# The general path of the experts moved two experts forward and shortened, x added in the last expert's turn, and the second block's tiles 32 bytes lower

## The chip, the cores and the metric

The kernel runs on one core of a Trainium2 chip. The metric is the time of one execution on the device in microseconds (us). It was measured three times before the change: 1717.10, 1709.79 and 1703.56 us, the median being 1709.79 us. One further execution was recorded by the hardware profiler; all rows below come from it.

## The reference: what is computed

The input is a sequence of 256 tokens with 1024 features in 32-bit floats. A first block applies a mixer, attention to a memory and a layer of 32 experts; a second block follows, of four SwiGLU layers ("ffn"), a recurrent layer and an attention layer. What matters here:

```python
for l in range(DEPTH):
    h = rmsnorm(x, norm_mix_g[l])
    x = x + parallel_mixer(h, ...)
    h = rmsnorm(x, norm_mem_g[l])
    x = x + memory_cross_attention(h, ...)
    h = rmsnorm(x, norm_ffn_g[l])
    x = x + hierarchical_moe(h, ...)      # each token: 2 of 32 experts
return rmsnorm(x, final_g)
# second block, D_FF = 2816, four times:
def swiglu(h, w13, w2):
    gate, up = jnp.split(h @ w13, 2, axis=-1)
    return (jax.nn.silu(gate) * up) @ w2
```

## The kernel before, in words

Features lie on partitions, tokens along the free dimension; x is kept as the tile `xT` of 8 chunks of 128 features by 256 tokens. The kernel writes the order of each engine's work out by hand, by the order of the Python statements; a tile framework adds the waits. SyncE's queue (SP) starts all the loads of weights, in program order.

**Products.** Most products are made of three matmuls in a reduced 32-bit format (`mm3`, L179 to L184): each factor is split into a high and a low part, and high by high (L182), high by low (L183) and low by high (L184) are added up. A weight tile of 1 MB (`raw`) is loaded, ScalarE (ACT) rounds it into `wh` (L159), and VectorE (DVE) subtracts that into `wl` (L160). The weights are the stationary operand of these matmuls, and 256 tokens of the activations the moving one: `xgh`/`xgl` are the normalised x, `hh`/`hl` the hidden features of an ffn (two buffers of each, in turn), `xkvh`/`xkvl` and `yh`/`yl` inputs of later layers.

**An ffn** (`ffn`, L1077) runs over 11 pieces of 256 hidden features (F = 2816): 48 matmuls into PSUM `A` from `xgh`/`xgl` (gate), 48 into `B` (up), and 48 from `hh`/`hl` into the sums `acc` (`rowproj`, L338). Four ffn make 4 x 11 x 48 = 2112 matmuls that read `hh` or `hl`.

**The experts** (`experts`, L812) run one after the other. Each has 32 slots for tokens out of each of two halves; its 6 MB of weights come in 6 tiles of 1 MB, 4 of `w_gu` and 2 of `w_down`, through a ring of 16 slots, the last eight loads through the 8 slots `raw` alone. In the turn of expert e TensorE (PE) makes gate and up of e (L938), adds the result of e-2 to the sums (`combine`, L979), transposes (L948) and makes the down product of e-1 (L964). In the turn of expert 24 (`e == NE - 8`), 16 full 32-bit matmuls by the identity (L887) add `xT` to `acc`.

**The general path.** A token can have more slots wanted than there are; then a flag `fi` is set, and a loop over all experts (`moe_over`, L982) computes what is missing. `rest` (L792 to L795) loads the flag on all engines and branches on it; with the inputs used here the path isn't taken. It stands behind the last `combine`. Ahead of it four loads of the second block's first weights are issued (`s.early`), which `wload` later picks up instead of loading.

**After the experts**, `after_moe` (L1025) makes two products of gains (`gg` L1030, `g2` L1032), then `xgh` on ACT (L226) and `xgl` on DVE (L227) out of the sums, with `gg`; then the first ffn starts.

Of the kernel before, what the change touches and what calls it, by code (L numbers as in the profile page):

```python
# [8 lines left out]
F32 = mybir.dt.float32  # L9
F32R = mybir.dt.float32r  # L10
I32 = mybir.dt.int32
AF = mybir.ActivationFunctionType
# [4 lines left out]
P = 128  # L17
T = 256
D = 1024
KC = D // P  # L20
EPS = 1e-6
F = 2816
NE = 32
# [24 lines left out]
class Block:  # L48
    def __init__(s, ctx, tc, io):
        s.tc, s.nc, s.ctx, s.io = tc, tc.nc, ctx, io  # L50
        s.n = s.turn = 0
        s.queue = s.behind = None
        s.early = []
        pool = lambda name, bufs, **k: ctx.enter_context(tc.tile_pool(name=name, bufs=bufs, **k))
        s.cp = pool("const", 1)
        s.wp = pool("weights", 3)
        s.tp = pool("temps", 2)
        s.xp = pool("x", 1)
        s.pa = pool("acc", 1, space=PSUM)
        s.pp = pool("ps", 2, space=PSUM)  # L60
# [76 lines left out]
    def wload(s, views, C, N, parts=1, between=None):  # L137

        nc = s.nc
        full = C * N == 2048  # L140
        early = s.early.pop(0) if s.early else None
        raw = s.new(s.wp, [P, 2048], "raw", F32, RAW) if early is None else early.rearrange("p c n -> p (c n)")
        wh = s.new(s.wp, [P, 2048], "wh", F32R, WHL)
        wl = s.new(s.wp, [P, 2048], "wl", F32R, WHL)
        v = lambda t: t[:, :C * N].rearrange("p (c n) -> p c n", n=N)
        if not isinstance(views, list):
            n = C // parts
            views = [views[:, i * n:(i + 1) * n] for i in range(parts)]
        c = 0
        for i, view in enumerate(views if early is None else []):  # L150
            nc.sync.dma_start(v(raw)[:, c:c + view.shape[1]], view)
            c += view.shape[1]
            if between is not None:
                between(i)
        cuts = max(parts, 2) if full else parts
        n = C * N // cuts
        for i in range(cuts):
            lo, hi = i * n, (i + 1) * n
            act = nc.scalar.copy(wh[:, lo:hi], raw[:, lo:hi])  # L159
            dve = nc.vector.tensor_sub(wl[:, lo:hi], raw[:, lo:hi], wh[:, lo:hi].bitcast(F32))  # L160
            if s.behind is not None:
                s.after(s.behind[0], act)
                s.after(s.behind[1], dve)
        return v(wh), v(wl)
# [611 lines left out]
        w4 = lambda a: a.unsqueeze(2).unsqueeze(3).to_broadcast(sh4)  # L776
        return pos, gs, gates, over, fi

    def moe(s, mt, xg, st, first):

        nc = s.nc
        s.mt = mt
        y = []

        def rows():
            y.append(s.rstd(s.colsum(st, s.bank()[1][:, 0:2]), D)[1])
            y.append(s.new(mt, [P, 2], "my"))
            nc.vector.tensor_copy(y[1], y[0])
            return y[0]
        pos, gs, gates, over, fi = s.route(xg, rows)  # L790
        with s.tc.tile_pool(name="experts", bufs=1) as me:
            def rest(acc):  # L792

                flag = nc.values_load(fi[0:1, 0:1], min_val=0, max_val=1)
                with s.tc.If(flag > 0):  # L795
                    s.moe_over(over, y[1], acc)
            acc = s.experts(me, pos, gs, gates, rest, first)
        return acc

    def tokens(s, xg, ks):  # L800
# [8 lines left out]
                        s.pe(s.nc.tensor.matmul(pt[:, h, j], src[:, k + j, h * P:(h + 1) * P], s.idr, start=True, stop=True))  # L809
                s.nc.scalar.copy(dst[:, :, k * P:(k + 2) * P], pt.rearrange("p h j b -> p h (j b)"))  # L810

    def experts(s, mt, pos, gs, gates, rest, first):  # L812
        nc = s.nc
        mm = nc.tensor.matmul

# [57 lines left out]
        acc = s.accs()  # L873
        for e in range(NE):
            i = e % 4
            if i == 0:
                now = nxt
                nxt = group(e + 4) if e + 4 < NE else None
            gx, rs = [x[i] for x in now[2]], slot[1][:, 1:2]
            ps = s.expert_in(e, gx)  # L880
            gu = s.new(mt, [P, 512], "gu", F32, 2)
            nc.scalar.mul(gu, ps, rs)
            if done is not None:
                s.combine(acc, *done)
            if e == NE - 8:
                for k in range(KC):
                    s.pe(mm(acc[k // 2][:, k % 2], s.ident, s.xT[:, k], start=False, stop=False))  # L887
            if nxt:
                gather(nxt, 2 * i)
            own = slot  # L890
            if e + 1 < NE:
                slot = slots(nxt if i == 3 else now, e + 1, (i + 1) % 4)
            hx = s.expert_act(mt, gu)
            if prev is not None:
                done = prev[0], s.expert_down(mt, *prev), prev[2]
            prev = (e, hx, *own)
        last = prev[0], s.expert_down(mt, *prev), prev[2]
        s.combine(acc, *done)
        s.combine(acc, *last)
        s.queue = None  # L900
        s.early = [s.wraw(view, KC, 256) for view in first]
        rest(acc)
        return acc

    def expert_loads(s):
# [76 lines left out]
    def moe_over(s, over, y, acc):  # L982

        nc, io, tc = s.nc, s.io, s.tc
        mm = nc.tensor.matmul
        with tc.tile_pool(name="over", bufs=1) as t:
            hT = s.new(s.mt, [P, KC, T], "tokh")
            r = s.spread(y, s.ps([P, T]))
            for k in range(KC):
                nc.vector.scalar_tensor_tensor(hT[:, k], s.xT[:, k], s.col("norm_ffn_g", k), r, op0=ALU.mult, op1=ALU.mult)  # L990
            for b in range(4):
                nc.scalar.copy(s.xT[:, 2 * b:2 * b + 2], acc[b])
            with tc.For_i(0, NE, 1) as e:
                dg = s.tmp([P, 2, P], "dg", 1)
# [4 lines left out]
                gb = s.new(t, [P, T], "ogb")  # L999
                nc.vector.tensor_copy(gb, pb)  # L1000
                row = lambda name, i: io[name][ds(e, 1), i].rearrange("o p c n -> p (o c) n")
                for c in range(4):
                    ps = s.ps([P, 2, T])
                    for n in range(2):
                        for i in range(4):
                            w = s.new(t, [P, 2, P], "ow", F32, 2)
                            nc.sync.dma_start(w, row("w_gu", i)[:, 2 * n:2 * n + 2, c * P:(c + 1) * P])
                            for j in range(2):
                                mm(ps[:, n], w[:, j], hT[:, 2 * i + j], start=i + j == 0, stop=i + j == 4)
                    hf = s.new(t, [P, T], "ohf")  # L1010
                    nc.scalar.activation(hf, ps[:, 0], AF.Silu)
                    nc.vector.tensor_mul(hf, hf, ps[:, 1])
                    nc.vector.tensor_mul(hf, hf, gb)
                    for i in range(2):
                        w = s.new(t, [P, 512], "owd")
                        nc.sync.dma_start(w, row("w_down", c // 2)[:, c % 2, i * 512:i * 512 + 512])
                        for m in range(4):
                            ps = s.ps([P, T])
                            mm(ps, w[:, m * P:(m + 1) * P], hf, start=True, stop=True)
                            nc.vector.tensor_add(s.xT[:, 4 * i + m], s.xT[:, 4 * i + m], ps)  # L1020
            for k in range(KC):
                mm(acc[k // 2][:, k % 2], s.ident, s.xT[:, k], start=k % 2 == 0, stop=k % 2 == 1)


    def after_moe(s, acc, p2):  # L1025


        nc = s.nc
        gg = s.new(p2, [P, KC], "gg")
        nc.vector.tensor_mul(gg, s.col("final_g", 0, 8), s.col("ffn1_norm_2", 0, 8))  # L1030
        g2 = s.new(p2, [P, KC], "g2")
        nc.vector.tensor_mul(g2, s.col("final_g", 0, 8), s.col("final_g", 0, 8))  # L1032
        xg = s.pair(s.xp, KC, "xg")
        for k in range(KC):
# [289 lines left out]
    def run(s):  # L1324
        tc, io = s.tc, s.io
        s.setup()
        with tc.tile_pool(name="first", bufs=1) as p1:
            s.cur = p1
            xg, rows, km, vm = s.mixer(p1)
            xg, st = s.mem_attention(p1, xg, rows, km, vm)  # L1330
        with tc.tile_pool(name="moe", bufs=1) as mt:
            w13 = io["ffn1_w13_2"][0]
            acc = s.moe(mt, xg, st, [w13[j] for j in (0, F // 256, 1, F // 256 + 1)])
# [19 lines left out]
RAW, WHL = 8, 3  # L1353
# [73 lines left out]
```

## Time and profile before

| | |
|---|---|
| median of 3 runs | 1709.79 us |
| the profiled execution | 1704.26 us |
| its span, first to last instruction | 1702.5 us |
| PE busy | 1655.3 us (97%) |
| DVE busy | 927.7 us (54%) |
| ACT busy | 704.4 us (41%) |
| mean granted clock of PE | 0.993 |

The span is the time from the first to the last instruction, 1.8 us less than that execution's own time. The granted clock is the share of full speed that the chip gave TensorE; it has two levels, 1.0 (2.4 GHz) and 0.5 (1.2 GHz). Experts fill about 246 to 709 us of the span, the second block the rest.

### The profile page before, as it was taken

The page shows a single profiled execution, that of the slowest core. Times are in us where ns is not written, and L with a number is a line of the kernel's source. Part 1 is how long each engine was busy: PE and PEld are TensorE (multiplying, and loading weights), DVE is VectorE, ACT ScalarE, POOL GpSimd, SP SyncE. Part 2 cuts the span into 40 slices and gives each one's busy share as a digit, 9 for nine tenths or more (in the row PEclk, how much of TensorE's full clock was granted, in tenths as well). Part 3 has the DMA queues.
Part 4 walks back from the last instruction along what each step waited for, and adds up shares of the span by engine and source line. Part 5 has one row for each costly group of instructions (what it writes and reads, how often), then busy time and mean ns, then how long its engine had stood idle before and what let it go on. Part 6 is the DMA issues. An engine that isn't in the chain of part 4 may idle for free.

```text
span 1702.5 us, 28058 instructions
## 1 busy us (share of the span) xinstructions
PE 1655.3 (97%) x11847; PEld 1350.5 (79%) x11847; DVE 927.7 (54%) x1636; ACT 704.4 (41%) x1138; POOL 5.0 (0%) x19
## 2 busy tenths in 40 slices
PE   8999999999999998799999999999999998999998
PEld 7878984444444443499999999999899997799998
DVE  7998651111111111385558875557655558875554
ACT  8525542111111111344346753436544346764342
POOL 0000000000000000000000000000000000000000
PEclk9999999999999999999999999999999999999999
DMA  9334369999999999865543555554655554135530
GB/s 363 137 124 177 127 251 387 420 419 419 419 420 419 420 420 419 360 264 198 177 158 138 225 215 179 187 186 144 220 182 192 179 192 155 50 125 192 181 123 26
DMA packets 60229, 408.03 MB, mean 240 GB/s; under 512 B 6595, under 2 KB 9923, under 8 KB 11459
## 3 DMA queue, kind: packets, MB, share of 16 engines
q1 hardware_dynamic: 60096, 406.18, 61.9%
q8 instruction: 95, 1.56, 0.4%
q14 instruction: 38, 0.29, 0.0%
HBM read 405.11 MB, written 1.05 MB: 239 GB/s over the span
## 4 chain that ended last, share of the span: by engine, by line
PE 54%; DVE 2%; ACT 1%; issue 0%; POOL 0%; ACTq 0%
PE acc L183 6%; PE A L183 6%; PE A L182 6%; PE acc L182 6%; PE A L184 6%; PE acc L184 6%; PE B L183 6%; PE B L182 6%; PE B L184 6%; DVE wl L160 1%; PE A L1285 1%; PE B L407 0%; ACT wh L159 0%; PE B L190 0%; PE A L190 0%
## 5 line engine op out<-in xcount | busy, mean ns | idle before, releaser
L159 ACT CAST wh<-raw 128x1024 fp32r<-128x1024 f32 (+2 forms) x378 | 377.9, 1035 | 425.5 <-issue 368.6
L160 DVE TENSOR_TENSOR wl<-raw,wh 128x1024 fp32r<-128x1024 f32 (+2 forms) x378 | 448.9, 1205 | 142.8 <-ACT wh L159 141.9
L182 PE MATMUL A<-xgh,wh 128*128 128x256 f32 (+1 forms) x872 | 246.1, 282 | 7.0 <-ACT xgh L226 7.0
L182 PE MATMUL B<-xgh,wh 128*128 128x256 f32 x872 | 245.4, 281 | 6.6 <-ACT wh L159 6.6
L183 PE MATMUL B<-xgl,wh 128*128 128x256 f32 x872 | 245.5, 282 | 0.0
L184 PE MATMUL B<-xgh,wl 128*128 128x256 f32 x872 | 245.5, 281 | 0.0
L183 PE MATMUL A<-xgl,wh 128*128 128x256 f32 (+1 forms) x872 | 245.4, 282 | 0.0
L184 PE MATMUL A<-xgh,wl 128*128 128x256 f32 (+1 forms) x872 | 244.8, 281 | 0.3 <-DVE wl L160 0.3
L183 PE MATMUL acc<-hl,wh 128*128 128x256 f32 x704 | 197.9, 282 | 0.2
L184 PE MATMUL acc<-hh,wl 128*128 128x256 f32 x704 | 197.9, 282 | 0.0
L182 PE MATMUL acc<-hh,wh 128*128 128x256 f32 x704 | 195.0, 282 | 0.1
L182 PEld LDWEIGHTS A<-xgh,wh 128*128 128x128 f32 (+1 forms) x872 | 164.4, 189 | 7.7 <-ACT xgh L226 7.5
L182 PEld LDWEIGHTS B<-xgh,wh 128*128 128x128 f32 x872 | 164.3, 188 | 7.5 <-ACT wh L159 6.9
L184 PEld LDWEIGHTS B<-xgh,wl 128*128 128x128 f32 x872 | 164.2, 188 | 1.5 <-DVE wl L160 0.9
L184 PEld LDWEIGHTS A<-xgh,wl 128*128 128x128 f32 (+1 forms) x872 | 164.3, 188 | 0.5 <-DVE wl L160 0.5
L183 PEld LDWEIGHTS A<-xgl,wh 128*128 128x128 f32 (+1 forms) x872 | 164.3, 188 | 0.5 <-DVE xgl L227 0.4
L183 PEld LDWEIGHTS B<-xgl,wh 128*128 128x128 f32 x872 | 164.4, 189 | 0.3
L848 DVE COPY gx<-B 128x128 f32<-128x128 f32 x64 | 18.6, 291 | 234.0 <-PE B L842 225.7
L938 PE MATMUL A<-raw,gx 128*64 128x512 f32 x560 | 128.0, 596 | 5.8 <-DMA raw<-in_w_gu_dram 5.8
L183 PEld LDWEIGHTS acc<-hl,wh 128*128 128x128 f32 x704 | 132.3, 188 | 0.6 <-DVE hl L225 0.6
L182 PEld LDWEIGHTS acc<-hh,wh 128*128 128x128 f32 x704 | 131.8, 189 | 1.0 <-ACT hh L225 0.7
L184 PEld LDWEIGHTS acc<-hh,wl 128*128 128x128 f32 x704 | 132.2, 188 | 0.0
(408 smaller groups left out, 2372.3 us busy)
## 6 DMA issues: line engine op xcount, KB each, us to landing
raw<-in_ffn_w_dram SPq DMA_DIRECT2D x132, 1024.0 KB, 4.8
raw<-in_w_gu_dram SPq DMA_DIRECT2D x70, 1024.0 KB, 19.9
raw<-in_w_down_dram SPq DMA_DIRECT2D x34, 1024.0 KB, 19.9
wh<-in_w_gu_dram SPq DMA_DIRECT2D x22, 1024.0 KB, 19.9
wl<-in_w_gu_dram SPq DMA_DIRECT2D x22, 1024.0 KB, 19.9
wh<-in_w_down_dram SPq DMA_DIRECT2D x11, 1024.0 KB, 19.9
wl<-in_w_down_dram SPq DMA_DIRECT2D x11, 1024.0 KB, 19.9
raw<-in_a_w_in_dram SPq DMA_DIRECT2D x8, 1024.0 KB, 5.0
```

The lines of the kernel that those rows point to most:

```text
L159: act = nc.scalar.copy(wh[:, lo:hi], raw[:, lo:hi])
L160: dve = nc.vector.tensor_sub(wl[:, lo:hi], raw[:, lo:hi], wh[:, lo:hi].bitcast(F32))
L182: s.pe(mm(out, w[0], x[0], start=first, stop=False))
L183: s.pe(mm(out, w[0], x[1], start=False, stop=False))
L184: s.pe(mm(out, w[1], x[0], start=False, stop=last))
L848: nc.vector.tensor_copy(dst, pg[:, :, i])
L938: s.pe(s.nc.tensor.matmul(ps[g * CAP:(g + 1) * CAP], gx[t // 2][:, 2 * (t % 2) + c], w[:, g, c * 512:c * 512 + 512], start=t + c == 0, sto ...
L1285: mm(sc[:, lo:lo + ke], qT[b:b + 64, c, qb * P:qb * P + P], kT[b:b + 64, c, 0:ke], start=True, stop=True)
```

## The change

1. `rest` is called at the end of the turn of expert 30 (`e == NE - 2`), behind the down product of expert 29, instead of behind the last `combine`. The four early loads vanish; the first loads of the second block are ordinary ones behind the conditional.
2. The general path is written as nested loops with fewer instructions (on PE 156 instead of some 470, counting each 32-bit matmul's two passes and their weight loads), adds into `xT` alone, and no longer copies the sums into `xT` and back.
3. The 16 matmuls that add `xT` to the sums (L884 in the new numbering) stand in the turn of expert 31 (`e == NE - 1`), between `combine` of expert 29 and the transposes. They come after the conditional, so that they carry what it may have added.
4. `g2`, 32 bytes a partition, is made in the pool of temporary tiles (tag `nr8`) and no longer in the pool `second`. Each later tile of `second`, and of the pools stacked on it, lies 32 bytes lower. Start addresses in bytes within a partition, as the two built programs have them:

| tile | before | mod 128 | after | mod 128 |
|---|---|---|---|---|
| hh (two) | 163712, 165760 | 0 | 163680, 165728 | 96 |
| hl (two) | 167808, 169856 | 0 | 167776, 169824 | 96 |
| xkvh, xkvl | 171904, 180096 | 0 | 171872, 180064 | 96 |
| yh, yl | 212960, 221152 | 96 | 212928, 221120 | 64 |
| xgh, xgl | 138816, 147008 | 64 | the same | 64 |
| wh (three) | 77344, 85536, 93728 | 32 | the same | 32 |
| wl (three) | 101920, 110112, 118304 | 32 | the same | 32 |

```diff
@@ wload
-        early = s.early.pop(0) if s.early else None
-        raw = s.new(s.wp, [P, 2048], "raw", F32, RAW) if early is None else early.rearrange("p c n -> p (c n)")
+        raw = s.new(s.wp, [P, 2048], "raw", F32, RAW)
...
@@ moe
-            def rest(acc):
+            def rest():
 
                 flag = nc.values_load(fi[0:1, 0:1], min_val=0, max_val=1)
                 with s.tc.If(flag > 0):
-                    s.moe_over(over, y[1], acc)
-            acc = s.experts(me, pos, gs, gates, rest, first)
+                    s.moe_over(over, y[1])
+            acc = s.experts(me, pos, gs, gates, rest)
@@ experts
-            if e == NE - 8:
+            if e == NE - 1:
                 for k in range(KC):
                     s.pe(mm(acc[k // 2][:, k % 2], s.ident, s.xT[:, k], start=False, stop=False))
...
             prev = (e, hx, *own)
+            if e == NE - 2:
+
+                rest()
+                s.queue = []
         last = prev[0], s.expert_down(mt, *prev), prev[2]
         s.combine(acc, *done)
         s.combine(acc, *last)
         s.queue = None
-        s.early = [s.wraw(view, KC, 256) for view in first]
-        rest(acc)
         return acc
@@ moe_over
-            for b in range(4):
-                nc.scalar.copy(s.xT[:, 2 * b:2 * b + 2], acc[b])
...
+                with tc.For_i(0, 2, 1) as u:
+                    with tc.For_i(0, 2, 1) as c:
+                        part(e, u, c)
...
-            for k in range(KC):
-                mm(acc[k // 2][:, k % 2], s.ident, s.xT[:, k], start=k % 2 == 0, stop=k % 2 == 1)
@@ after_moe
-        g2 = s.new(p2, [P, KC], "g2")
+        g2 = s.tmp([P, KC], "nr8", 1)
```

PE's order at the conditional, before. L979 is the last `combine`, L794 and L795 the flag and the branch, L182 the second block's first matmul; between lies the general path.

```order
L979 MATMUL acc_2782<-oT_5557,yl_5654 128x256
L979 MATMUL acc_2784<-oT_5557,yl_5654 128x256
L794 TENSOR_LOAD fi_2660
L795 COMPARE_AND_BRANCH
...
L1022 MATMUL acc_2781<-xT,ident 128x256 x2
L1022 MATMUL acc_2782<-xT,ident 128x256 x2
L1022 MATMUL acc_2783<-xT,ident 128x256 x2
L1022 MATMUL acc_2784<-xT,ident 128x256 x2
L795 UNCONDITIONAL_BRANCH x2
L182 MATMUL A_6052<-xgh_6034,wh_6054 128x256
L183 MATMUL A_6052<-xgl_6035,wh_6054 128x256
```

After: the conditional stands between the down product of expert 29 (L963) and gate and up of expert 31 (L937), and the `xT` matmuls (L884) two steps behind it.

```order
L963 MATMUL A_5562<-raw_5366,hx_5482 64x512 x4
L963 MATMUL A_5562<-raw_5372,hx_5482 64x512 x4
L791 TENSOR_LOAD fi_2660
L792 COMPARE_AND_BRANCH
...
L792 UNCONDITIONAL_BRANCH
L937 MATMUL A_5719<-raw_5489,gx_5035 64x512 x4
...
L884 MATMUL acc_2781<-xT,ident 128x256 x2
L884 MATMUL acc_2782<-xT,ident 128x256 x2
L884 MATMUL acc_2783<-xT,ident 128x256 x2
L884 MATMUL acc_2784<-xT,ident 128x256 x2
L947 MATMUL A_5762<-ident,gu_5736 128x128 x4
```

So nothing stands any more between the last `combine` and L182, and what follows the branch on PE is now the 16 matmuls of expert 31.

DVE's order at the same place before: `yl` (L969) of the last expert, the first `wl`, the branch, and only then `gg` and the first `xgl`.

```order
L969 SCALAR_TENSOR_TENSOR yl_5641<-A_5631,gt_5481,yh_5640 128x512
L969 SCALAR_TENSOR_TENSOR yl_5654<-A_5644,gt_5559,yh_5653 128x512
L160 TENSOR_TENSOR wl_6055<-raw_5689,wh_6054 128x1024 x2
L794 TENSOR_LOAD fi_2660
L795 COMPARE_AND_BRANCH
...
L795 UNCONDITIONAL_BRANCH x2
L1030 TENSOR_TENSOR gg_6030<-par 128x8
L1032 TENSOR_TENSOR g_1136_6032<-par 128x8
L227 SCALAR_TENSOR_TENSOR xgl_6035<-acc_2781,gg_6030,xgh_6034 128x256
```

After:

```order
L951 TENSOR_TENSOR hx_5560<-sl_5558,A_5553 128x256
L968 SCALAR_TENSOR_TENSOR yl_5576<-A_5562,gt_5407,yh_5575 128x512
L791 TENSOR_LOAD fi_2660
L792 COMPARE_AND_BRANCH
...
L792 UNCONDITIONAL_BRANCH
L1038 TENSOR_TENSOR gg_5834<-par 128x8
L951 TENSOR_TENSOR hx_5769<-sl_5767,A_5762 128x256
L968 SCALAR_TENSOR_TENSOR yl_5781<-A_5771,gt_5473,yh_5780 128x512
L968 SCALAR_TENSOR_TENSOR yl_5794<-A_5784,gt_5551,yh_5793 128x512
L158 TENSOR_TENSOR wl_5860<-raw_5858,wh_5859 128x1024 x2
L225 SCALAR_TENSOR_TENSOR xgl_5839<-acc_2781,gg_5834,xgh_5838 128x256
```

`gg` now follows the branch directly, ahead of the last `hx` and the last two `yl`, and `wl` is followed by `xgl` without a branch between.

SP's order before: the last two loads of the experts, the four early ones, the branch, and the first ordinary load (L151).

```order
L176 DMA raw_5575<-in_w_down_dram 128x2048
L176 DMA raw_5581<-in_w_down_dram 128x2048
L176 DMA raw_5689<-in_ffn_w_2_dram 128x2048
L176 DMA raw_5691<-in_ffn_w_2_dram 128x2048
L176 DMA raw_5693<-in_ffn_w_2_dram 128x2048
L176 DMA raw_5695<-in_ffn_w_2_dram 128x2048
L794 TENSOR_LOAD fi_2660
L795 COMPARE_AND_BRANCH
...
L795 UNCONDITIONAL_BRANCH x2
L794 ISA x2
L151 DMA raw_6361<-in_ffn_w_2_dram 128x2048
```

After:

```order
L174 DMA raw_5567<-in_w_down_dram 128x2048
L174 DMA raw_5573<-in_w_down_dram 128x2048
L791 TENSOR_LOAD fi_2660
L792 COMPARE_AND_BRANCH
...
L792 UNCONDITIONAL_BRANCH
L791 ISA x2
L149 DMA raw_5858<-in_ffn_w_2_dram 128x2048
L149 DMA raw_5914<-in_ffn_w_2_dram 128x2048
```

The first loads of the second block are now issued behind SP's branch, and the branch stands behind the experts' last load as before.

## Rows read from the trace of the kernel before

**Rows 1.** Windows: start and end us, length, busy by engine, granted PE clock, DMA share, GB/s

```profile
core 0: us, PE busy (x) PEld busy (x) DVE busy (x) ACT busy (x) POOL busy (x), PEclk, DMA share, GB/s
640.00:660.00 20.00, 18.44 (x98) 6.61 (x96) 2.27 (x5) 2.82 (x5) 0.00 (x0) 1.00 1.01 421
714.06:720.88 6.82, 5.04 (x22) 4.81 (x23) 4.96 (x15) 5.57 (x13) 0.12 (x1) 0.50 0.66 210
760.00:800.00 40.00, 40.00 (x341) 40.00 (x341) 23.81 (x25) 16.61 (x19) 0.00 (x0) 1.00 0.50 183
246.40:253.20 6.80, 6.07 (x22) 5.07 (x23) 4.98 (x19) 1.07 (x4) 0.00 (x0) 0.50 1.01 418
```

**Rows 2.** Timeline of PE, expert 31 to the second block: start us, us, what, idle before

```profile
687.43 1.94 PE L938 MATMUL A<-raw,gx 128*64 128x512 f32 x8
...
694.83 1.94 PE L938 MATMUL A<-raw,gx 128*64 128x512 f32 x8 [0.56 <-DMA raw<-in_w_gu_dram]
...
698.42 3.65 PE L964 MATMUL A<-raw,hx 128*64 128x512 f32 x16
702.40 1.94 PE L964 MATMUL A<-raw,hx 128*64 128x512 f32 x8 [0.33 <-SPq L795]
704.80 1.94 PE L964 MATMUL A<-raw,hx 128*64 128x512 f32 x8 [0.46 <-SPq L795]
...
708.31 0.73 PE L979 MATMUL acc<-oT,yl 64*128 64x256 f32 x8
715.84 0.58 PE L182 MATMUL A<-xgh,wh 128*128 128x256 f32 x1 [6.79 <-ACT xgh L226]
```

**Rows 3.** Instructions of line L795, the branch, on the sequencers: duration ns min/median/max, start us

```profile
L795 SPq EVENT_SEMAPHORE  x8: 17/17/17, 700.1 to 714.7; - x8
...
L795 PEldq COMPARE_BRANCH  x1: 5672/5672/5672, 709.2 to 709.2; - x1
```

**Rows 4.** DMA queues from 712 to 714 us: packets, MB, share

```profile
q8 instruction: 1, 0.02, 3.4%
```

**Rows 5.** Timeline of DVE around the same places

```profile
688.34 0.75 DVE L969 SCALAR_TENSOR_TENSOR yl<-A,gt,yh 128x512 fp32r<-128x512 f32 x1 [3.48 <-ACT yh L968]
...
708.44 2.36 DVE L160 TENSOR_TENSOR wl<-raw,wh 128x1024 fp32r<-128x1024 f32 x2 [0.18 <-ACT wh L159]
714.98 0.17 DVE L1030 TENSOR_TENSOR gg<-par 128x8 f32<-128x8 f32 x1 [4.18 <-PEq L795]
715.82 1.66 DVE L227 SCALAR_TENSOR_TENSOR xgl<-acc,gg,xgh 128x256 fp32r<-128x256 f32 x4 [0.59 <-ACT xgh L226]
```

**Rows 6.** Timeline of PE at the matmuls that add x (expert 24's turn)

```profile
591.60 3.72 PE L887 MATMUL acc<-xT,ident 128*128 128x256 f32 x16
594.97 0.59 PE L842 MATMUL B<-oh,tokh 128*128 128x256 f32 x2
```

**Rows 7.** Timeline of PE in the second block: starts 48 matmuls apart

```profile
1663.53 0.28 PE L182 MATMUL B<-xgh,wh 128*128 128x256 f32 x1
...
1669.18 0.28 PE L182 MATMUL acc<-hh,wh 128*128 128x256 f32 x1
...
1674.94 0.28 PE L182 MATMUL A<-xgh,wh 128*128 128x256 f32 x1
...
968.38 0.28 PE L182 MATMUL acc<-yh,wh 128*128 128x256 f32 x1
...
973.82 0.28 PE L182 MATMUL acc<-yh,wh 128*128 128x256 f32 x1
```

**Rows 8.** Groups by line, 710 to 1703 us: count, busy us and mean ns, idle before

```profile
L182 PE MATMUL acc<-hh,wh 128*128 128x256 f32 x704 | 195.0, 282 | 0.1
L182 PE MATMUL acc<-yh,wh 128*128 128x256 f32 x64 | 17.7, 276 | 0.0
L182 PE MATMUL acc<-xkvh,wh 128*128 128x256 f32 x64 | 17.5, 300 | 0.0
```

**Rows 9.** Timeline of PE: two gaps in the experts' stretch

```profile
246.53 0.36 PE L737 MATMUL B<-ow,up 128*128 128x32 f32 x1 [2.17 <-DVE w L756]
...
665.06 1.94 PE L938 MATMUL A<-xgl,gx 128*64 128x512 f32 x8 [1.33 <-DMA xgl<-in_w_gu_dram]
```

More of the change, by code (lines that the diff above doesn't have):

```diff
@@ L52, in __init__ @@
         s.queue = s.behind = None
-        s.early = []
         pool = lambda name, bufs, **k: ctx.enter_context(tc.tile_pool(name=name, bufs=bufs, **k))
@@ L149, in wload @@
         c = 0
-        for i, view in enumerate(views if early is None else []):
+        for i, view in enumerate(views):
             nc.sync.dma_start(v(raw)[:, c:c + view.shape[1]], view)
@@ L777, in route, with moe @@
         return pos, gs, gates, over, fi
-    def moe(s, mt, xg, st, first):
+    def moe(s, mt, xg, st):
         nc = s.nc
@@ L810, in tokens, with experts @@
                 s.nc.scalar.copy(dst[:, :, k * P:(k + 2) * P], pt.rearrange("p h j b -> p h (j b)"))
-    def experts(s, mt, pos, gs, gates, rest, first):
+    def experts(s, mt, pos, gs, gates, rest):
         nc = s.nc
@@ L980, in combine, with moe_over @@
                             start=e == 0 and i == 0 and m % 2 == 0, stop=e == NE - 1 and i == 1 and m % 2 == 1))
-    def moe_over(s, over, y, acc):
+    def moe_over(s, over, y):
         nc, io, tc = s.nc, s.io, s.tc
@@ L990, in moe_over, with part @@
                 nc.vector.scalar_tensor_tensor(hT[:, k], s.xT[:, k], s.col("norm_ffn_g", k), r, op0=ALU.mult, op1=ALU.mult)
-            for b in range(4):
-                nc.scalar.copy(s.xT[:, 2 * b:2 * b + 2], acc[b])
+            wg = io["w_gu"].rearrange("e i p n c -> (e i) p n c")
+            wd = io["w_down"].rearrange("e t p c n -> (e t) p c n")
+            gb = s.new(t, [P, T], "ogb")
+            def part(e, u, c):
+                ga = s.new(t, [P, 2, T], "oga")
+                nc.vector.memset(ga, 0.0)
+                with tc.For_i(0, 4, 1) as i:
+                    hk = s.new(t, [P, 2, T], "ohk")
+                    nc.vector.tensor_copy(hk, hT[:, ds(i * 2, 2)])
+                    for n in range(2):
+                        w = s.new(t, [P, 2, P], "ow", F32, 2)
+                        nc.sync.dma_start(w, wg[ds(e * 4 + i, 1), :, 2 * n:2 * n + 2, ds(u * 2 * P + c * P, P)].rearrange("o p n c -> p (o n) c"))
+                        ps = s.ps([P, T])
+                        for j in range(2):
+                            mm(ps, w[:, j], hk[:, j], start=j == 0, stop=j == 1)
+                        nc.vector.tensor_add(ga[:, n], ga[:, n], ps)
+                hf = s.new(t, [P, T], "ohf")
+                nc.scalar.activation(hf, ga[:, 0], AF.Silu)
+                nc.vector.tensor_mul(hf, hf, ga[:, 1])
+                nc.vector.tensor_mul(hf, hf, gb)
+                for i in range(2):
+                    w = s.new(t, [P, 512], "owd")
+                    nc.sync.dma_start(w, wd[ds(e * 2 + u, 1), :, ds(c, 1), i * 512:i * 512 + 512].rearrange("o p c n -> p (o c n)"))
+                    for m in range(4):
+                        ps = s.ps([P, T])
+                        mm(ps, w[:, m * P:(m + 1) * P], hf, start=True, stop=True)
+                        nc.vector.tensor_add(s.xT[:, 4 * i + m], s.xT[:, 4 * i + m], ps)
             with tc.For_i(0, NE, 1) as e:
@@ L998, in moe_over @@
                     mm(pb[:, h * P:(h + 1) * P], s.ones, dg[:, h], start=True, stop=True)
-                gb = s.new(t, [P, T], "ogb")
                 nc.vector.tensor_copy(gb, pb)
[L1001 to L1020, printed above, removed]
-            for k in range(KC):
-                mm(acc[k // 2][:, k % 2], s.ident, s.xT[:, k], start=k % 2 == 0, stop=k % 2 == 1)
+                with tc.For_i(0, 2, 1) as u:
+                    with tc.For_i(0, 2, 1) as c:
+                        part(e, u, c)
     def after_moe(s, acc, p2):
@@ L1331, in run @@
         with tc.tile_pool(name="moe", bufs=1) as mt:
-            w13 = io["ffn1_w13_2"][0]
-            acc = s.moe(mt, xg, st, [w13[j] for j in (0, F // 256, 1, F // 256 + 1)])
+            acc = s.moe(mt, xg, st)
         with tc.tile_pool(name="second", bufs=1) as p2:
```

## The prediction

> **What bounds the kernel now.** I read the windows first, then PE's timeline, then single lines. In the experts' stretch the DMA engines are full (share 1.01, 421 GB/s) and PE waits a little for each weight tile; in the second block PE is busy for 40.00 of 40.00 us at full clock while DMA stands at half [rows 1]. So a microsecond of PE saved among the experts is lost to the next landing, and one saved in the second block comes off the end. Between the two lies the conditional. PE's timeline shows its last combine at 708.31 for 0.73, so to 709.04, and the next matmul at 715.84 after 6.79 us of idle time [rows 2]. PE's own branch instruction took 5672 ns [rows 3], and while it stood there one packet moved on q8, the queue that brings instructions [rows 4]. DVE's `gg` waited for PE's sequencer until 714.98 and the first `xgl` began at 715.82 [rows 5]. From 714.06 to 720.88 the granted clock was 0.50, the lower level, with PE busy for 5.04 us of it [rows 1]. SP too stood at the branch: its eight semaphore events run from 700.1 to 714.7 [rows 3], the landings of the loads that it had outstanding.
>
> **The 32 bytes.** Rows 7 are starts 48 matmuls apart, in code that differs in the moving operand alone. From `xgh`: 1669.18 - 1663.53 = 5.65 us, 117.7 ns each. From `hh`: 1674.94 - 1669.18 = 5.76 us, 120.0 ns. From `yh`: 973.82 - 968.38 = 5.44 us, 113.3 ns [rows 7]. The weights go through the same three slots in each, the shapes are one shape, and PE has no idle time in any. What differs is where the operand starts: `hh` at 0 past a multiple of 128 bytes, `xgh` at 64, `yh` at 96. The change puts `hh` and `hl` at 96. My reading is that the place sets the pace, so that they will run like `yh`. The count is 3 x 704 = 2112 matmuls [rows 8]; 2112 x 6.7 ns = 14.1 us, all in the stretch that PE bounds. Two small groups move with them: `xkvh`/`xkvl`, from 0 to 96, 192 matmuls [rows 8], as `hh`: -1.3; `yh`/`yl`, from 96 to 64, 192 matmuls at 117.7 in place of 113.3: +0.8. Sum: -14.6 us. The bounds are nothing (a pace that belongs to the tile, not to its place) and, upwards, 2.1 us for each nanosecond that the new place costs more. The value between, the pace of `xgh`, gives 2112 x 2.3 = -4.9. I take -14.6 because `yh` lies at exactly the new offset with the same weights.
>
> All these paces are for matmuls that wait for nothing, and they differ. The Trainium skill (SBUF — State Buffer, "Operand start alignment") asks only that an operand start at a multiple of its element size, says that this is about legality and not about speed, and adds under "SBUF: two separate sides" that the port of PE never waits on anyone. By that page the 32 bytes would be worth 0 in place of -14.6; the page timed nothing there, and the 6.7 ns between `hh` and `yh` speak against it.
>
> **The conditional in its new place.** On PE the branch now follows the down product of expert 29, which ends where gate and up of 31 starts now, at 687.43 [rows 2]. What follows the branch waits for DVE to have passed its own, and DVE has `yl` of expert 29 ahead of it, 688.34 + 0.75 = 689.09 [rows 5]. So PE resumes at about 689.3, 1.9 us late. Its four tiles need some 1.8 us each (3.65 for sixteen matmuls), and the last starts at 694.83, after a wait for its landing [rows 2]; 689.3 + 3 x 1.8 = 694.7 is before that, so the delay is used up and costs nothing. The cover is the full DMA queue; without it the price would be 1.9.
>
> The risk is the clock. After 2.17 us of idle time at 246.53 PE ran at 0.50 from 246.40 to 253.20; after 1.33 at 665.06 it did not [rows 1, 9]. 1.9 lies between, nearer the first. If it falls for 6.8 us, two tiles take 3.6 each and two 1.8: 689.3 + 10.8 = 700.1 in place of 696.6, +3.5, less 0.8 of slack behind it (0.33 + 0.46 of idle time ahead of the two last down products [rows 2]): +2.7. I take 0, since the idle time falls short of the 2.17.
>
> SP's branch stands where it did, behind the last expert load, and its way past holds it until the loads outstanding there have landed, the last tile of gate and up at 694.8 [rows 2]. The second block's loads come behind that, at about 694.9. The queue is not empty by then: the four down tiles fill it until about 704.8 [rows 2], so the four early loads are not missed: 0, covered by 10 us. DVE's `gg` now waits for SP to about 694.9 and what stands behind it, the last `hx`, is due after the transposes of expert 31, some three microseconds later: 0. On POOL nothing follows until the end of the experts: 0. The shorter loops are not run: 0, but for the length jumped over (the second rival).
>
> **x into the sums.** 594.97 - 591.60 = 3.37 us for the 16 matmuls [rows 6]. In expert 24's turn the next landing hid them, and taking them out there gains nothing. In expert 31's turn only the 0.8 of slack is left to hide them, so everything after is 2.6 later: the last combine ends at 711.6.
>
> **The second block's start.** Behind the last `yl` DVE makes `wl`, 708.44 + 2.36 = 710.80 [rows 5]; moved by 2.6 it ends at 713.4. With no branch and `gg` long made, `xgl` follows at 713.4 in place of 715.82: -2.4. PE waits about 2 us there in place of 6.79. Should the clock then not fall, up to half of the 5.04 us at 0.50 comes back as well, -2.5, as far as DVE and ACT keep up. Between -2.4 and -4.9 I take -2.4, the gap being nearly as long as the one at 246.53.
>
> **The sum.** -14.6 - 2.4 = -17.0. The profiled execution's 1704.26 becomes 1687.3; it stands 5.5 below the median of the three, so the forecast is 1709.79 - 17.0 = **1692.8 us**.
>
> **Rivals.**
>
> *The address is worth little* (chance 0.31). The pace may hang on something else that goes with the tile: which engine wrote it last, or its distance from the weights. For it: all the evidence is from other tiles, and only one of them, `yh`, runs at 113.3. Against it: in the same stretch, with the same code, `hh` is slower than `xgh` each time. Only the conditional's -2.4 is left: 1707.4; with the pace of `xgh`, -2.4 - 4.9 (and without the two small groups): 1702.5.
>
> *PE's branch stalls again* (0.10). The 5672 ns with a packet on q8 [rows 3, 4] show that PE had to fetch what it jumped to. Now it jumps over about a third as much, which speaks for a target that is already there; but the fetch would meet a full DMA queue [rows 1]. PE would resume at 687.5 + 5.7 = 693.2, four tiles take it to 700.4 in place of 696.6, +3.8 less 0.8 = +3.0, and at the lower clock some 3.5 more. With the address as forecast: 1695.8 to 1699.3, middle 1697.5. The Trainium skill (Runtime: NRT & Kernel Launch, "Instruction fetch mechanics") has such a fetch whenever a taken branch leaves the two blocks of 256 instructions held; the 5672 ns agree, and the some 156 instructions now jumped over could still reach into a block that isn't held.
>
> *The new place is slower* (0.07), the one that ends on the other side. Offset 96 may be good for `yh` by its distance from something else, and bad for `hh`. It decides the sign from 2.4 / 2.112 = 1.1 ns above 120.0. A step as large as the one hoped for, 6.7 ns up, costs 14.1 and gives 1709.79 + 14.1 - 2.4 = 1721.5. For it: no row shows `hh` anywhere but at 0. Against it: at 0 it is already the slowest of the three.
>
> **How the numbers follow.** The forecast has 0.52; its own range, with the clock kept (-2.5) or lost (+2.7) and some 4 us for the spread of the runs around their median, is 1686 to 1699. About 1% of the time, 17.1 us, is what a measurement of this kernel can tell from no change, so the line for faster is 1692.7, through the middle of the forecast. I give a little more than half of it to faster, since more of the open ends lie below: 0.30, and 0.06 more for a conditional worth more than I took or a place better than `yh`'s. Slower by over 1% needs the third rival at nearly 130 ns: 0.04. The rest, 0.60, is within 1%. The range takes in the first rival up to its upper value and leaves out the third: 1683 to 1708.
>
> **What would show it.** Of the profile of the changed kernel: 48 matmuls from `hh` in 5.44 us (right), 5.65 or 5.76 (wrong); those from `xkvh` as fast, those from `yh` at 5.65. PE idle for about 1.9 us ahead of expert 31, its branch short, the clock there at 1.00, gate and up still ending near 696.6. The `xT` matmuls 3.4 us long behind the combine, the last combine ending near 711.6. `xgl` directly behind `wl` near 713.4. I would be wrong if the pace of `hh` stayed at 120.0, if a packet on q8 came with a long branch on PE, or if another tile that moved by 32 bytes got slower by as much as `hh` got faster.

## The result and the profile after

The changed kernel took 1694.61 us (median of 9 runs, 1689.32 to 1703.13) against 1705.45 us before (9 runs, 1703.13 to 1717.23): a ratio of 0.993 with a 95% interval of 0.9906 to 0.9955. It is faster by 10.8 us or 0.7%, inside the range of the forecast, on the side of "within 1%". The profiled execution took 1691.88 us (1704.26 before), its span 1690.1 us.

Windows, as in [rows 1]: the first is gate and up of expert 31, the second the start of the second block, then the second block's middle, then the start of the attention layer.

```profile
690.33:699.04 8.71, 8.71 (x32) 3.12 (x33) 0.17 (x1) 0.00 (x0) 0.00 (x0) 0.80 1.01 413
714.00:721.00 7.00, 5.30 (x40) 4.90 (x41) 6.89 (x15) 6.59 (x14) 0.00 (x0) 1.00 1.02 423
760.00:800.00 40.00, 40.00 (x343) 40.00 (x342) 23.43 (x25) 17.12 (x20) 0.00 (x0) 1.00 0.54 183
1435.00:1442.00 7.00, 5.19 (x23) 3.85 (x23) 5.82 (x11) 5.10 (x9) 0.00 (x0) 0.53 0.00 0
1442.00:1449.00 7.00, 6.02 (x33) 3.54 (x30) 6.49 (x13) 5.03 (x12) 0.00 (x0) 0.99 0.44 150
```

In this execution the lower clock that stood at the second block's start before is gone (1.00), and some of it has appeared among the experts (0.80 on average behind the branch). PE is as full as before in the second block and yet issues a little more in the same 40 us.

PE's timeline, answering to [rows 2]:

```profile
684.38 3.65 PE L963 MATMUL A<-raw,hx 128*64 128x512 f32 x16
690.33 8.79 PE L937 MATMUL A<-raw,gx 128*64 128x512 f32 x32 [2.29 <-DVEq L792]
699.04 0.75 PE L978 MATMUL acc<-oT,yh 64*128 64x256 f32 x8
...
700.19 3.72 PE L884 MATMUL acc<-xT,ident 128*128 128x256 f32 x16
703.75 0.60 PE L947 MATMUL A<-ident,gu 128*128 128x128 f32 x4
704.27 7.09 PE L963 MATMUL A<-raw,hx 128*64 128x512 f32 x32
...
712.94 0.74 PE L978 MATMUL acc<-oT,yl 64*128 64x256 f32 x8
714.41 0.38 PE L180 MATMUL A<-xgh,wh 128*128 128x256 f32 x1 [0.73 <-ACT xgh L224]
715.88 0.38 PE L181 MATMUL A<-xgl,wh 128*128 128x256 f32 x1 [1.09 <-DVE xgl L225]
```

The branch on the sequencers [rows 3], and DVE around it [rows 5]:

```profile
L792 SPq EVENT_SEMAPHORE  x4: 17/17/17, 694.4 to 695.2; - x4
L792 PEldq COMPARE_BRANCH  x1: 368/368/368, 686.1 to 686.1; - x1
...
L792 DVEq EVENT_SEMAPHORE  x1: 21/21/21, 690.2 to 690.2; - x1
```

```profile
688.80 0.75 DVE L968 SCALAR_TENSOR_TENSOR yl<-A,gt,yh 128x512 fp32r<-128x512 f32 x1 [3.48 <-ACT yh L967]
690.58 0.17 DVE L1038 TENSOR_TENSOR gg<-par 128x8 f32<-128x8 f32 x1 [1.02 <-DMA raw<-in_w_gu_dram]
...
713.07 2.36 DVE L158 TENSOR_TENSOR wl<-raw,wh 128x1024 fp32r<-128x1024 f32 x2 [0.18 <-ACT wh L157]
715.34 2.83 DVE L225 SCALAR_TENSOR_TENSOR xgl<-acc,gg,xgh 128x256 fp32r<-128x256 f32 x7
```

PE's branch takes 368 ns in place of 5672. PE then waits for DVE, whose event comes 0.65 us after `yl` ends (688.80 + 0.75 = 689.55), so the gap is 2.29 us. At the second block `xgl` follows `wl` without a break.

Starts 48 matmuls apart, as in [rows 7], twice in the first ffn:

```profile
775.35 0.28 PE L180 MATMUL acc<-hh,wh 128*128 128x256 f32 x1
...
781.01 0.28 PE L180 MATMUL A<-xgh,wh 128*128 128x256 f32 x1
...
792.52 0.28 PE L180 MATMUL acc<-hh,wh 128*128 128x256 f32 x1
...
797.97 0.28 PE L180 MATMUL A<-xgh,wh 128*128 128x256 f32 x1
```

Each group is 48 matmuls from `hh` and `hl`, up to the next one from `xgh`. The same tiles at the same offsets: 5.66 us (117.9 ns each), and 17 us later 5.45 (113.5 ns). Before, each such group took 5.76 [rows 7]. So the pace is not a property of the offset alone. Over all 2112 matmuls the steps between neighbouring starts have a mean of 115.5 ns, and of 119.9 before.

### The profile page after: what moved, and what is told of

Same layout as the page of the kernel before. It is cut to its first block, busy times and chain, and to the rows that moved or that the text cites. A ratio compares the mean times of both kernels' runs of the same rounds, so it can differ in the third digit from the quotient of the medians.

```text
span 1690.1 us, 28047 instructions
## 1 busy us (share of the span) xinstructions
PE 1646.4 (97%) x11847; PEld 1339.6 (79%) x11847; DVE 927.1 (55%) x1636; ACT 704.8 (42%) x1138; POOL 5.0 (0%) x19
## 4 chain that ended last, share of the span: by engine, by line
PE 53%; DVE 3%; ACT 2%; issue 1%; ACTq 0%
PE A L181 6%; PE A L180 6%; PE A L182 6%; PE acc L181 5%; PE acc L180 5%; PE acc L182 5%; PE B L180 5%; PE B L181 5%; PE B L182 5%; DVE wl L158 1%; ACT wh L157 1%; PE A L1293 1%; PE A L937 1%; PE B L405 0%; PE A L963 0%
## 5 line engine op out<-in xcount | busy, mean ns | idle before, releaser
L182 PE MATMUL B<-xgh,wl 128*128 128x256 f32 x872 | 245.7, 282 | 0.0
L182 PE MATMUL A<-xgh,wl 128*128 128x256 f32 (+1 forms) x872 | 243.9, 280 | 0.4 <-DVE wl L158 0.4
L182 PE MATMUL acc<-hh,wl 128*128 128x256 f32 x704 | 194.5, 278 | 0.0
L182 PEld LDWEIGHTS B<-xgh,wl 128*128 128x128 f32 x872 | 164.5, 189 | 1.5 <-DVE wl L158 0.9
L182 PEld LDWEIGHTS A<-xgh,wl 128*128 128x128 f32 (+1 forms) x872 | 163.5, 187 | 0.6 <-DVE wl L158 0.6
L937 PE MATMUL A<-raw,gx 128*64 128x512 f32 x560 | 130.2, 603 | 7.7 <-DMA raw<-in_w_gu_dram 5.4
L182 PEld LDWEIGHTS acc<-hh,wl 128*128 128x128 f32 x704 | 132.2, 188 | 0.0
```

What stands on the lines that cost most here:

```text
L182: s.pe(mm(out, w[1], x[0], start=False, stop=last))
L937: s.pe(s.nc.tensor.matmul(ps[g * CAP:(g + 1) * CAP], gx[t // 2][:, 2 * (t % 2) + c], w[:, g, c * 512:c * 512 + 512], start=t + c == 0, sto ...
```

## The experiments

All times are medians; ratios are to the kernel before on the same chip, with their 95% interval. The runs stand in three sessions, on three chips, whose medians of the kernel before are 1705.83, 1705.65 and 1705.41 us: the first four experiments belong to the first, the next four to the second, the last four kernels to the third. Paces and clocks come from one profiled execution of each kernel.

**The address alone.** In the kernel before:

```diff
-        g2 = s.new(p2, [P, KC], "g2")
+        g2 = s.tmp([P, KC], "nr8", 1)
```

> The kernel before with g2 alone moved: hh, hl and the tiles above lie 32 bytes lower, the conditional and x stay where they were. Theory A (the start address of the moving operand sets the pace, the profile after shows 115.4 ns a matmul from hh/hl in place of 119.9): about 2112 x 4.4 = 9.3 us less, some 1696 us, with PE still idle for 6.8 us ahead of the second block. Theory B (the gain came from the conditional, the address only shuffles paces from run to run): within 3 us of the kernel before.

1699.41 us, 0.9957 (0.9944 to 0.9971), 6.4 us less; the pace of `hh`/`hl` fell to 115.9 ns. Theory B, that the address only shuffles paces from run to run, is out; but 3 us are missing, and windows of the attention layer show where they can have gone. First the kernel before, then this one:

```profile
1442.00:1449.00 7.00, 3.16 (x15) 2.49 (x15) 6.86 (x16) 5.10 (x10) 0.00 (x0) 0.68 0.11 46
1449.00:1456.00 7.00, 6.36 (x33) 3.74 (x32) 5.22 (x11) 5.20 (x13) 0.00 (x0) 0.83 0.27 69
```

```profile
1435.00:1442.00 7.00, 3.39 (x12) 2.37 (x13) 6.76 (x18) 5.11 (x10) 0.00 (x0) 0.64 0.19 81
1442.00:1449.00 7.00, 6.36 (x24) 3.74 (x22) 4.86 (x8) 4.01 (x9) 0.00 (x0) 0.50 0.19 39
1449.00:1456.00 7.00, 6.61 (x20) 4.06 (x19) 4.28 (x10) 3.39 (x8) 0.00 (x0) 0.50 0.27 114
1456.00:1463.00 7.00, 6.82 (x35) 4.51 (x36) 4.46 (x10) 5.96 (x15) 0.00 (x0) 0.90 0.00 0
```

With two levels, 1.00 and 0.50, a window's mean tells how long the lower one stood: a mean of 0.64 over 7 us is 0.36 / 0.50 x 7 = 5.0 us. So the clock was at 0.50 for some 20 us here, against some 7 us in the kernel before and in the changed kernel (0.53 and 0.99 above). It fell at the same two idle stretches of PE, which in the changed kernel are

```profile
1435.10 0.30 PE L1241 MATMUL A<-ident,qk 128*128 128x128 f32 x1 [3.63 <-DVE qk L1232]
1438.81 0.90 PE L1241 MATMUL A<-ident,qk 128*128 128x128 f32 x3 [1.71 <-DVE qk L1232]
```

The mean granted clock of an execution follows this stay. Of the ten profiled executions without the unread matmuls of a later experiment, the four at 0.993 to 0.995 have 6.8 us at 0.50 there, five at 0.989 or 0.990 have 20.5 to 23.9, and the one at 0.986 has 37.6. All twelve runs of this kernel lie at 0.987 to 0.990.

**The conditional and x alone.** In the changed kernel:

```diff
-        g2 = s.tmp([P, KC], "nr8", 1)
+        g2 = s.new(p2, [P, KC], "g2")
```

> The changed kernel with g2 back in its pool: hh at 0 past a multiple of 128 again, the conditional and x moved. Theory A: hh/hl at 119.9 ns as before, and only the conditional's part, 1 to 4 us less than before, some 1703 us. Theory B: all of the 10 us, some 1695 us.

1706.74 us, 0.9997 (0.9979 to 1.0015): no gain in the median. The pace of `hh` is 119.9 ns again. The twelve runs fall in two groups by their mean granted clock: five at 0.994 or 0.995, 1699.99 to 1702.54 us, and seven at 0.991 or below, 1706.70 to 1712.57 us. The first group stands near the forecast of theory A, and no run comes near the 1695 us of theory B; the median mixes in the attention's clock.

**`xgh` given the weights' remainder.** In the changed kernel:

```diff
-        gg = s.new(p2, [P, KC], "gg")
+        gg = s.tmp([P, KC], "nr8b", 1)
```

> The changed kernel with gg too among the temporary tiles under a tag of its own: xgh/xgl lie 32 bytes higher (96 past a multiple of 128, the weights' remainder of 64), hh stays. Theory A in the form that equal remainders of 64 of moving operand and weights give the steady 113 to 118 ns: xgh/xgl, 117.0 ns now, go to between 113.4 and 117.8, up to 4608 x 3.6 = 17 us less than the changed kernel, some 1680 to 1695 us. Theory A in the form that only hh matters, or theory B: like the changed kernel, 1692 to 1697 us.

1705.13 us, 0.9984 (0.9963 to 1.0006): a miss of both ranges. All of `xgh`, `xgl`, `hh` and `hl` run at 117.8 ns, steadily, with few exceptions; in the second ffn 48 matmuls take 5.65 us:

```profile
1061.93 0.28 PE L180 MATMUL acc<-hh,wh 128*128 128x256 f32 x1
...
1067.58 0.28 PE L180 MATMUL A<-xgh,wh 128*128 128x256 f32 x1
```

Equal remainders give a steady pace, but here not the low one. The attention's clock is in the median too: eleven of the twelve runs have a mean granted clock of 0.991 or below, and the one at 0.995 took 1697.68 us.

**The weights moved as well.** In the changed kernel:

```diff
         s.cp = pool("const", 1)
+        s.tc.nc.vector.memset(s.cp.tile([P, 8], F32, name="pad0"), 0.0)
```

> The changed kernel with 32 bytes put ahead of the weights' tiles: wh and wl now at 64 past a multiple of 128, hh at 0, xgh at 96. If only the moving operand's own place counts: hh at 0 runs at 119.9 ns again, 9 us more than the changed kernel. If its place relative to the weights counts (equal remainders of 64 for hh and the weights, unequal for xgh): hh keeps 113 to 118 ns, and xgh, unequal, stays near 117 ns; the time stays at 1692 to 1698 us.

1697.52 us, 0.9943 (0.9923 to 0.9963). The 32 bytes shift every tile behind them too, so all distances between operands and weights are those of the changed kernel. `hh` starts at 0 past a multiple of 128 here, as it did before the change, and its pace is that of the changed kernel, 115.5 ns. PE's timeline of this kernel, in the second ffn, has 5.44 us:

```profile
1060.73 0.28 PE L181 MATMUL acc<-hh,wh 128*128 128x256 f32 x1
...
1066.17 0.28 PE L181 MATMUL A<-xgh,wh 128*128 128x256 f32 x1
```

and of the kernel with the conditional alone, `hh` at 0 as well, 5.76 us:

```profile
1063.37 0.28 PE L180 MATMUL acc<-hh,wh 128*128 128x256 f32 x1
...
1069.13 0.28 PE L180 MATMUL A<-xgh,wh 128*128 128x256 f32 x1
```

So it is the place relative to the weights that counts, not the operand's own. These two kernels also give the worth of it on one chip: the two runs of this one at a mean granted clock of 0.994 or more took 1691.81 and 1693.02 us, the five of the other 1699.99 to 1702.54, some 9 us more.

**The changed kernel once more**, unaltered.

> The changed kernel unaltered, profiled and timed once more. Theory C (where the operand's and the weights' remainders of 64 are equal, the pace locks onto 113.4 or 117.8 ns for a whole ffn, and which one it is depends on how the stretch was entered): the four ffn of this profile show the same two paces, but not necessarily the same choice in each as the first profile (which was 113.4 mid-way in the first, 117.8 in the second, 113.4 in the third and fourth). Rival: the program fixes the choice, and the sequence repeats exactly. Time 1689 to 1703 us; at a mean granted clock of 0.993 or more, about 1692 us.

1695.56 us, 0.9927 (0.9902 to 0.9953). In the second ffn the first profile of the kernel has 5.66 us for 48,

```profile
1061.25 0.28 PE L180 MATMUL acc<-hh,wh 128*128 128x256 f32 x1
...
1066.91 0.28 PE L180 MATMUL A<-xgh,wh 128*128 128x256 f32 x1
```

and this one 5.44:

```profile
1060.09 0.28 PE L180 MATMUL acc<-hh,wh 128*128 128x256 f32 x1
...
1065.53 0.28 PE L180 MATMUL A<-xgh,wh 128*128 128x256 f32 x1
```

All eight groups of 48 between the ends of that ffn agree, in either profile. In the fourth ffn it is the other way round, 113.4 ns first and 117.8 now. The first and the third ffn repeat: three groups and one group at 117.8 ns, then 113.4. Theory C holds in the second and the fourth: one program, two executions, another choice. What makes the choice is not shown; the record does not say whether the two ran on one chip.

**The conditional behind gate and up of expert 31.** In the changed kernel:

```diff
             ps = s.expert_in(e, gx)
+            if e == NE - 1:
+                rest()
+                s.queue = []
...
-            if e == NE - 2:
-
-                rest()
-                s.queue = []
```

> The changed kernel with the conditional moved on behind gate and up of expert 31, ahead of the combine of expert 29, so that DVE has passed its branch long before PE comes to its own. If the 2.29 us of idle time and the lower clock behind it among the experts come from DVE's late branch: PE idle for under 1 us at the branch, granted clock 1.00 there, the last combine 1 to 3 us earlier counted from the start of the experts. If PE's own branch is what costs: the same gap at the new place. The total moves by 3 us at most.

1693.15 us, 0.9917 (0.9893 to 0.9941). The window over gate and up and PE's timeline behind the branch:

```profile
688.00:699.00 11.00, 10.05 (x56) 4.55 (x55) 0.92 (x2) 1.37 (x2) 0.00 (x0) 1.00 1.01 414
```

```profile
697.66 3.69 PE L887 MATMUL acc<-xT,ident 128*128 128x256 f32 x16 [0.16 <-PEq L792]
```

PE idles for 0.16 us at the branch (and 0.79 us ahead of gate and up, for `yh`), the clock stays at 1.00, and the last combine comes 464.05 us after the experts' first matmul in place of 466.35. The idle time came from DVE's late branch. (The scheduler also put `combine` of 29 between the tiles of gate and up here.) Only 0.8 of the 2.3 us is left when the first 96 matmuls of the second block are done, since the clock falls at the block's start in this profile (0.76 from 714 to 721 us).

The lower clock does not always follow that idle time. Nine profiled executions have the conditional at the end of expert 30's turn and PE idle for 2.29 or 2.30 us behind it. In six the clock falls there; in three (the conditional and x alone, `xgh` given the weights' remainder, the weights moved as well) it stays at 1.00, and falls at the start of the second block instead. The first of the three:

```profile
691.11 7.09 PE L937 MATMUL A<-raw,gx 128*64 128x512 f32 x32 [2.29 <-DVEq L792]
```

With the same wait, gate and up take 7.09 us here and 8.79 in the first profile of the changed kernel.

**PE kept busy in the attention layer.** In the changed kernel, 14 and 6 matmuls before the second transposes of the queries:

```diff
-    def to_channels(s, dst, src, c0, c1, g):
+    def to_channels(s, dst, src, c0, c1, g, fill=None):
...
             pt = s.ps([P, 2, T])
+            if fill is not None:
+                t = s.pa.tile([P, 512], F32, name=s.nm("fill"), tag="acc0")
+                for i in range(14 if c == 0 else 6):
+                    nc.tensor.matmul(t, fill[:, 0, 0:P], fill[:, 0:2], start=True, stop=True)
...
-            s.to_channels(qT, qA, 4 * n, 4 * n + 4, gq)
+            s.to_channels(qT, qA, 4 * n, 4 * n + 4, gq, xg[0] if n else None)
```

> The changed kernel with 20 matmuls whose result nobody reads put into the two idle stretches of PE (3.6 and 1.7 us) at the start of the attention layer. Theory D (the runs of one kernel differ by how long the granted clock stays at 0.50 behind these two stretches, 5 us in the first profile of the changed kernel and over 20 in that of the kernel with the address alone): the clock stays at 1.00 there, the upper runs vanish, spread under 5 us, median about 1689 us, 3 us below the fastest cluster of the changed kernel. Rival (the spread comes from the paces of the ffn): median and spread as for the changed kernel.

1690.90 us, 0.9902 (0.9879 to 0.9926), runs from 1687.93 to 1693.56. The windows of the same place:

```profile
1432.00:1439.00 7.00, 6.39 (x35) 4.48 (x34) 6.59 (x23) 6.97 (x13) 0.00 (x0) 1.00 0.44 150
1439.00:1446.00 7.00, 6.17 (x37) 3.79 (x36) 7.00 (x14) 6.44 (x15) 0.00 (x0) 1.00 0.01 2
```

The clock stays at 1.00 and the upper runs are gone. Theory D holds. The choice of paces could make the spread that remains: one ffn at the other pace is 528 x 4.4 ns = 2.3 us; that is not shown. The median came 2 us above the figure expected, and the spread of 5.6 us is a little over the 5 expected.

**x back in expert 24's turn.** In the changed kernel:

```diff
-            if e == NE - 1:
+            if e == NE - 8:
                 for k in range(KC):
```

> The changed kernel with the 16 matmuls that add x put back into the turn of expert 24; it leaves out that they carry what a general path behind them would add to x, which isn't taken here. If they cost what the forecast has (3.4 us less 0.8 of slack): the last combine 2.6 us earlier, the second block's start as much; if the start of the second block is set by DVE's casts alone, less than 1 us of it shows there.

1694.35 us, 0.9931 (0.9906 to 0.9956). Counted from the experts' first matmul the last combine is 3.28 us earlier (463.07 in place of 466.35), and so is the second block's start: the whole of the 16 matmuls, no slack hid any. The expected 2.6 fell short; the medians, 1694.35 against 1695.56 us on the same chip, are too spread to show the 3.3.

**The change without the attention's clock.** The kernel before with the same unread matmuls, and the changed kernel with them and `g2` back in its pool (both edits are shown above).

> The kernel before with the same 20 unread matmuls in the attention layer's idle stretches. With that source of spread gone, the median should be 1 to 2 us below the fastest cluster of the kernel before (1703 to 1705 us), some 1702 us, and the difference to the changed kernel with the same matmuls (1690.9 us) is the worth of the change without the attention's clock: about 11 to 12 us (theory D). If the spread had another source, the runs reach up to 1712 us as before.

> The changed kernel with the unread matmuls and with g2 back in its pool, so hh at 0 past a multiple of 128. Its difference to the changed kernel with the unread matmuls (1690.9 us) is the worth of the 32 bytes alone: 2112 x 4.4 ns = 9.3 us, some 1700 us; its difference to the kernel before with them is the conditional and x, 2 to 4 us.

1703.21 us (12 runs, 1701.61 to 1704.22; 0.9976, 0.9963 to 0.9990) and 1700.69 us (12 runs, 1699.01 to 1703.67; 0.9962, 0.9948 to 0.9976). The runs that reached 1716.18 us without the unread matmuls are gone. With the changed kernel's 1690.90 that makes 2.5 us for the conditional and x, 9.8 for the 32 bytes, 12.3 together. The 2.5 stands between two kernels on one chip (some 1 us either way); the 1690.90 is from the session before, on another chip, where the kernel before took 0.24 us more, and the 9.8 (some 2 us either way) carries that besides. The profiles agree: 2112 x 4.4 = 9.3 us in the pace, and from the experts' first matmul to the end of the second block's first 96 the eight executions with the conditional and x moved as in the change take 480.15 to 482.58 us, 481.1 on average, against 483.75 to 483.88 in the three with neither moved, 2.7 us less.

**All at remainder 0.** The edit ahead of the weights and that of `gg`, together.

> The changed kernel with the weights 32 bytes higher, xgh/xgl 64 higher and hh 32 higher, so that all three have remainder 0 of 64. Theory C: all paces equal and steady, locked onto one of the two values; as in the kernel with all three at 32, where it was 117.8 nearly everywhere, 1698 to 1710 us. If remainder 0 itself were good, or the lock fell on 113.4 this time: 2112 + 4608 matmuls at 3.5 to 4.4 ns less, down to 1670 us.

1699.62 us, 0.9947 (0.9922 to 0.9972), runs from 1689.66 to 1707.13. As in the kernel with all at 32, `hh` and `xgh` run at 117.8 ns nearly throughout in the profiled execution (1704.99 us). The time lies in the range expected, 5.5 us under that of its twin at 32, which the attention's clock could make; it isn't settled. The three runs at a mean granted clock of 0.994 or more took 1689.66 to 1693.17 us, as those of the changed kernel did, so other executions may well have had the lower pace.

**The best version.** The conditional behind gate and up of 31, and the unread matmuls.

> The conditional behind gate and up of expert 31 and the unread matmuls in the attention layer together: if the two gains are independent, 1 to 2 us less than with the unread matmuls alone, some 1689.5 us, with a spread under 6 us; if the first gain is lost at DVE's casts, 1691 us.

1687.21 us (1685.44 to 1688.84), 0.9874 (0.9852 to 0.9897): faster than both kernels, and 2.3 us below the figure expected, though the kernel that the figure was reckoned from ran on another chip.

## Why the prediction was right, and where it was not

- **The 32 bytes: the mechanism held in part, the term was mis-sized.** I had -14.6 us with the two small groups, measured -9.8. The step that failed is "the place sets the pace, so that they will run like `yh`": it is the place relative to the weights, and it sets two paces. What the runs show is that with equal remainders of 64 in moving operand and weights the pace settles on 113.4 or 117.8 ns and keeps to it, often for a whole ffn; in two of the four ffn which of them differs from one execution to the next. `yh` had shown me the lower alone. Half and half over 2112 matmuls, 119.9 - 115.5 = 4.4 ns make 9.3 us. The rival "worth little", which named the distance from the weights as the possible cause, had the cause; its price came out too small. `xgl`, which did not move, went from 117.8 to 117.1 ns between the two profiles, 1.2 us over 1728 matmuls that I had no term for.
- **The two small groups**: `xkvh`/`xkvl` went from 119.4 to 117.7, `yh`/`yl` from 113.4 to 117.4, together +0.4 us where I had -0.5. `yh` lost nearly what `hh` gained, by the same rule: its remainder is now unequal. I had named that as a sign of being wrong, and it was one for the reading by the operand's own place.
- **"This is about legality, not speed"** (the Trainium skill, SBUF — State Buffer, "Operand start alignment"), read as a forecast, would have made this 0. 1700.69 against 1690.90 us, with 32 bytes the only difference between the two kernels, speaks against reading it so for PE; the page says that it timed nothing.
- **The conditional: right sum, wrong parts, which is luck.** -2.4 forecast, -2.5 measured. The gap among the experts is 2.29 us and not 1.9, because I ended DVE's part with `yl` and left out its own load of the flag and branch, 0.65 us. In six of nine profiles the clock then fell: the window behind it shows 0.80, and the 32 matmuls took 8.71 us where four times 1.8 was counted. In the other three they took the 7.1 that was counted, and gate and up ended 0.0 to 1.1 us later than before, counted from the experts' first matmul: there the loads nearly covered the wait, as I had it. So the step "I take 0, since the idle time falls short of the 2.17" failed on both counts: the idle time did not fall short, and its length alone does not decide. x cost 3.3 and not 2.6, since the slack I subtracted was already used up by that delay (704.27 to 711.29 shows both down products without a break). The last combine came 4.1 us later, where I had 2.6. Against this, PE idled 0.73 and 1.09 us ahead of the second block, in two pieces and not the 2 in one that I had, and the clock stayed at 1.00 there in this profile: 7.0 us less from the last combine to the end of the block's first 96 matmuls, where I had 5.0 to 7.5. From the experts' first matmul it is 480.96 us in place of 483.88.
- **SP, POOL, the early loads and `gg`**: 0 each, as forecast. SP passed at 695.2, `gg` was made at 690.58, without the wait for SP to 694.9 that I had, and the DMA share stays at 1.01 to 1.02.
- **PE's branch** did not stall (368 ns). It took 228 to 373 ns in the eleven profiled executions with the new general path and 5472 to 5672 in the three with the old one; whether that is for the shorter path or for the new place, no run tells apart.
- **What I did not see**: two idle stretches of PE in the attention layer, after which the clock is low for a time that differs between executions. It can account for the 10.8 us between the medians being less than the 12.3 of the parts: in the nine runs of the changed kernel four have a mean granted clock of 0.993 or more (1689.32 to 1693.91 us), five 0.986 to 0.990 (1694.61 to 1703.13).
- **The time itself was close by luck.** 1692.8 us was forecast and 1694.61 measured because two errors nearly cancel: the start of the sum, 1709.79, was the median of three runs, 4.3 us above the 1705.45 of nine; and the change was put at 17.0 us, 6.2 more than the 10.8 measured.

## What to carry to other kernels

Compare the start-to-start step of equal matmuls in one trace before you call a stretch of a full PE finished; here 32 bytes of a start address were worth four times what moving a conditional was. When a step is moved to where PE must wait for another engine, count all that engine does up to the release, its branch and flag load too. And where medians spread by more than the effect, find what the executions differ in, take that away in both kernels, and then compare.

## What the runs showed of the hardware that was not expected

- The step between 256-column matmuls with 128x128 weights depends on how the start of the moving operand lies to that of the weights: with equal remainders of 64 bytes, 113.4 or 117.8 ns, steady; with remainders 32 apart, irregular from step to step, with means of 116.9 to 120.2 ns. In every equal case the distance was 64 past a multiple of 128; a whole multiple of 128 was not run. The unequal ones part as well: `xgh`/`xgl` and `yh`/`yl` at a distance of 32 past a multiple of 128 had 116.9 to 119.0 ns, `hh`/`hl` and `xkvh`/`xkvl` at 96 had 119.3 to 120.2. With all operands equal it was 117.8 nearly always in the one profiled execution of each of the two such kernels; in the others the low pace appeared in `hh` with stretches of unequal operands between its groups. How a stretch is caught in one of the two paces, the runs don't show, nor why.
- The stay of the granted clock at 0.50 behind the same idle stretches (3.6 and 1.5 to 1.7 us) was 6.8 us in one execution, 20.5 in another and 37.6 in a third, with PE busy for 32.6 of the 37.6. 20 matmuls that nobody reads put an end to it, and took 2.2 us off the median even of the kernel before (1705.41 to 1703.21).
- An idle stretch of 2.29 us brought the clock down in six of nine executions and not in three, with the same matmuls ahead of it.
